# Down projections of both layers as seven products of half operands, with sums of the weights made beforehand

## The chip, the core and the metric

The kernel runs on one core of one Trainium2 chip. The metric is the device time of the whole program in microseconds; the median of several runs is compared. Single executions of one kernel agree within a few tenths of a per cent. Engines are named as the profile names them: PE (TensorE matmuls) with PEld (its weight loads), DVE (VectorE), ACT (ScalarE), POOL (GpSimd) and SP (SyncE, which here only issues DMA transfers).

## What is computed

One inference step of a two-layer network for two groups of requests, in float32: a prompt of 1024 tokens and 8 samples of 16 tokens, 1152 columns in all, with 1024 features. Layer 0 is an RWKV-7 time mixing, layer 1 a banded attention; behind each stands a SwiGLU feed-forward. Only the feed-forwards matter here:

```python
def swiglu(h, w_gate, w_up, w_down):
    return (jax.nn.silu(h @ w_gate) * (h @ w_up)) @ w_down
...
        h = modulate(rms_norm(x, p['norm_ffn'][l]), sh_f, sc_f)
        x = x + gt_f[:, None, :] * swiglu(h, p['w_gate'][l], p['w_up'][l], p['w_down'][l])
```

The inner width D_FF is 2816, that is 22 blocks of 128; `w_gate` and `w_up` are 1024 x 2816, `w_down` is 2816 x 1024. The modulations (shift, scale, gate of every sub-layer) come from `silu(c) @ w_ada + b_ada`.

## The kernel before

Features lie on the 128 partitions, tokens in the columns. The columns are split into two token groups, c = 0 with 512 and c = 1 with 640. A float32 product is made of three matmuls (`mm3`, line 143 issues each): both operands are split into a high part (ACT, L272) and the rest (DVE, L273), and high x high, high x rest and rest x high are added in PSUM. Weights are loaded raw by SP into a tile `rq` (five buffers), then split into a pair of tiles `w` (sixteen buffers, eight pairs).

The gate and up projections (`gate_up`, called from `ffn` for each of the 22 blocks f) already use seven products in place of eight: input features, tokens and output features (gate, up) are halved, sums of the weight quarters are formed on POOL (L1340 to L1343 in `strassen_weights`), and the products are added up on ACT, DVE and POOL (helper `add`, L1369), with L1376 and L1380 on ACT and L1383 and L1385 on DVE. Each product is a PSUM tile of 576 columns, 256 of group 0 and 320 of group 1, in half-groups of tokens. There are three such wide PSUM tiles (two `S`, one `PT`). The two results of a block, s0 and s1 (first and second half of each group's tokens), go to DRAM (`sd`, L1390).

The down projection (the second half of `ffn`) then runs over the 22 blocks in 11 pairs p, for c = 0 and 1 and for 8 blocks n of output features: six matmuls of 512 columns, or twelve of 320, give one PSUM tile that is added to a running sum in SBUF (L1436). The pair of blocks is read back from `sd` (L1411) and split; `w_down` is loaded and split in halves (L249). For the last pairs the gate and the residual are applied (L1170) in place of the addition, and the result is stored (L1440). In layer 0 the steps of `ada_steps` (modulations 12 to 27, loads at L260, matmuls from tile `h` with `scT`) run between the pairs, and `done` starts the next norm for each group as soon as it is ready; in layer 1 the down projection is the end of the program.

The engines' queues are in order. Which instruction stands where in each queue is decided when the program is built, by a scheduler with its own estimates; a tile with one buffer is handed on when its last reader has finished, a DMA included.

Of the kernel before, what the change touches and what calls it, by code (L numbers as in the profile page):

```python
# [8 lines left out]
F32 = mybir.dt.float32  # L9
F32R = mybir.dt.float32r  # L10
AF = mybir.ActivationFunctionType
ALU = mybir.AluOpType
# [64 lines left out]
def prep(i):  # L77
    i = {k: np.asarray(v) for k, v in i.items()}
    d = {}
    d["cst"] = _CST  # L80
    d["ti"] = _solver_identity()
    t = np.arange(384)
    rs = np.stack([t % 64 != 0, np.where(t < 256, t % 64, t % 16) != 0]).astype(np.float32)
    d["rs"] = np.ascontiguousarray(np.broadcast_to(rs[:, None], (2, 128, 384)))
    x = np.concatenate([i["x_prompt"][0], i["x_sample"].reshape(128, 1024)], 0)
# [5 lines left out]
    c = np.zeros((32, 1024), np.float32)  # L91
# [13 lines left out]
    st = i["state_wkv"][0].transpose(3, 1, 0, 2)  # L105
    st = st.reshape(64, 8, 2, 8, 64).transpose(2, 0, 1, 3, 4)
# [18 lines left out]
    q, u = np.arange(128)[:, None], np.arange(256)[None, :]  # L125
# [5 lines left out]
    for l in range(2):  # L131
        d[f"wg{l}"] = _tiles(i["w_gate"][l])
        d[f"wu{l}"] = _tiles(i["w_up"][l])
        d[f"wd{l}"] = i["w_down"][l].reshape(22, 128, 1024)
    return {k: np.ascontiguousarray(v) for k, v in d.items()}


# [8 lines left out]
class Trunk:  # L146
# [372 lines left out]
    def spill(self, n, b, f, t):  # L519
        self.nc.sync.dma_start(self.sp[b][n][:, :, f, :], t.rearrange("p (w t) -> p w t", t=128))  # L520
# [826 lines left out]
        yield put(a21)  # L1347
        yield put(a22)

    def gate_up(self, sd, B, W, cs):  # L1350

        nc = self.nc
        dve = nc.vector
        gp = nc.gpsimd
# [28 lines left out]
        dve.tensor_tensor(s1, s1, t5, ALU.mult)  # L1383
        add(dve, u3, product(3), u3)
        dve.tensor_tensor(s0, s0, u3, ALU.mult)  # L1385
        for h, s in enumerate((s0, s1)):
            for c in cs:
                o, n = 256 * c - n0, (256, 320)[c]
                t0 = 512 * c + n * h
                nc.sync.dma_start(sd[:, t0:t0 + n], s[:, o:o + n])  # L1390

    def ffn(self, l, B, W, part1, xsrc, dst, done):

        nc = self.nc
        sd = [self.dp.tile([128, 2, 1152], F32, name=f"sd{l}_{p}") for p in range(11)]
        self.gate_up(sd[0][:, 0], B, iter(W), (0,))
        for _ in part1:
            pass
        self.gate_up(sd[0][:, 0], B, iter(W), (1,))
        for f in range(1, 22):  # L1400
            self.gate_up(sd[f // 2][:, f % 2], B, self.strassen_weights(l, f, nc.vector if f == 1 else None), (0, 1))
        self.ada = self.ada_steps(range(12, 28), "acc", 1) if l == 0 else iter(())
        gate = 48 * l + 40
        acc, end = {}, iter(())
        act, W = {}, {}

        def begin(p):
            for c in range(2):
                w = (512, 640)[c]
                raw, hi, lo = (self.slot(c, dt)[:, :2 * w].rearrange("p (i t) -> p i t", i=2) for dt in (F32, F32R, F32R))  # L1410
                nc.sync.dma_start(raw, sd[p][:, :, self.cols(c)])  # L1411
                self.split(hi, lo, raw)
                act[p, c] = hi, lo
            W[p] = [self.halves(self.a[f"wd{l}"][f]) for f in (2 * p, 2 * p + 1)]
            self.step(7)

        for p, c in [(p, c) for p in range(9) for c in range(2)] + [(9, 1), (10, 1), (9, 0), (10, 0)]:
                if (p, c) not in act:
                    begin(p)
                if p == 0:  # L1420
                    acc[c] = self.feats(c)
                if p == 10:
                    st = self.sq_open()
                for n in range(8):
                    ns = slice(n % 4 * 128, (n % 4 + 1) * 128)
                    d, parts = self.pz(c)
                    for z, o, m in parts:
                        for i in range(2):
                            wh, wl = W[p][i][n // 4]
                            hi, lo = (act[p, c][h][:, i, o:o + m] for h in range(2))  # L1430
                            self.mm3(z, wh[:, ns], wl[:, ns], hi, lo, i == 0, i == 1)
                    y = acc[c][n]
                    if p == 0:
                        nc.scalar.activation(y, d, AF.Copy)
                    elif p <= 7:
                        nc.vector.tensor_tensor(y, y, d, ALU.add)  # L1436
                    else:
                        self.residual(512, n, gate, y, y, d)
                    if p == 10:
                        nc.sync.dma_start(dst[:, n, self.cols(c)], y)  # L1440
                        if l == 0:
                            self.sq_add(st, y, n < 6)
                    if p == 7:
                        x = self.ev("xin")[:, :y.shape[-1]]
                        nc.sync.dma_start(x, xsrc[:, n, self.cols(c)])
                        self.residual(512, n, gate, y, x, y)
                    next(end, None)
                if p == 10:
                    for _ in end:
                        pass  # L1450
                    end = done(c, acc[c], st)
        return end

    def dense(self, x2, x3, close):
# [531 lines left out]
```

## Time and profile before

| | us |
|---|---|
| median of 3 runs (3802.68 to 3817.41) | 3810.66 |
| the profiled execution | 3804.49 |
| its span | 3802.7 |
| busy in the span: PE | 3506.1 (92%) |
| DVE | 2263.6 (60%) |
| ACT | 1573.8 (41%) |
| POOL | 591.6 (16%) |

The busy shares are means over stages with different limits. The program has the time mixing up to about 1300 us, layer 0's gate/up stage from there to 1797 us, its down stage to about 2150 us, keys, values and attention to about 3000 us, layer 1's gate/up stage to 3520 us and its down stage to the end. Rows of a timeline give start, length, engine, line, operation, output<-inputs and shape, and in brackets the idle time before with what ended it. "DMA to landing" is the time from the start of the issue on SP to the moment at which the data are there.

### The profile page before, as it was taken

The numbers are of one execution on the slowest core, as the hardware profiler recorded it, in microseconds if no ns is written. First come the engines' busy times: TensorE is split into PE (matmuls) and PEld (weight loads), VectorE is DVE, ScalarE is ACT, GpSimd is POOL, SyncE is SP. The second block draws the span as 40 slices with busy tenths as digits, with TensorE's granted clock in tenths as the row PEclk, the third lists the DMA queues.
The fourth block names the chain that finished last, engine by engine and source line by source line (L and its number), as shares of the span: only waits on it lengthen the run. The fifth ranks groups of instructions, "written<-read, shape, count | busy, mean of one in ns | idle before, by whom it ended". The sixth has DMA issues, their size and how long they took to land.

```text
span 3802.7 us, 72100 instructions
## 1 busy us (share of the span) xinstructions
PE 3506.1 (92%) x28550; PEld 3098.0 (81%) x28550; DVE 2263.6 (60%) x4396; ACT 1573.8 (41%) x3006; POOL 591.6 (16%) x497
## 2 busy tenths in 40 slices
PE   5889989989999799999999899789889799999999
PEld 4777778777667699999888879667677799999898
DVE  4666667765445854554457742666565755545667
ACT  5545546544223533333311452556554533333310
POOL 0000000000011154453000100000000255444000
PEclk9887899899699899999999999899899899999999
DMA  5876776776665322224654122554565322222521
GB/s 212 236 216 170 207 220 184 201 203 201 192 197 176 113 84 76 76 73 157 221 177 172 64 71 92 153 151 155 152 203 178 120 78 71 76 75 96 171 86 66
DMA packets 426995, 554.01 MB, mean 146 GB/s; under 512 B 128385, under 2 KB 292737, under 8 KB 422177
## 3 DMA queue, kind: packets, MB, share of 16 engines
q1 hardware_dynamic: 351344, 450.68, 36.9%
q0 software_dynamic: 22224, 80.36, 6.9%
q10 hardware_dynamic: 53088, 18.36, 2.1%
q8 instruction: 225, 3.69, 0.4%
q14 instruction: 114, 0.93, 0.1%
HBM read 415.85 MB, written 133.40 MB: 144 GB/s over the span
## 4 chain that ended last, share of the span: by engine, by line
PE 69%; DMA 11%; DVE 10%; issue 4%; ACT 4%; SPq 1%; ACTq 0%; POOL 0%; DVEq 0%; POOLq 0%
PE S L143 32%; PE PT L143 15%; PE acc L143 12%; PE st L143 3%; PE O L143 2%; PE G L143 1%; DVE h L273 1%; PE aux L143 1%; PE PT L1811 1%; PE Y L143 1%; DMA TT<-Z 1%; DMA h<-out_kT 1%; DVE wlo L273 1%; DMA raw<-in_rw_o 1%; DMA h<-in_wo 1%
## 5 line engine op out<-in xcount | busy, mean ns | idle before, releaser
L143 PE MATMUL S<-h,w 128*128 128x320 f32 (+1 forms) x4944 | 689.7, 298 | 12.3 <-ACT h L272 4.8
L143 PEld LDWEIGHTS S<-h,w 128*128 128x128 f32 x4944 | 671.8, 191 | 18.4 <-ACT h L272 5.6
L143 PE MATMUL S<-h,wh 128*128 128x320 f32 (+1 forms) x2844 | 529.8, 338 | 15.9 <-DVE h L1170 6.8
L143 PE MATMUL acc<-mx,whi 128*128 128x384 f32 x1728 | 508.5, 372 | 32.7 <-ACT whi L272 13.0
L143 PEld LDWEIGHTS S<-h,wh 128*128 128x128 f32 x2844 | 456.1, 189 | 70.8 <-issue 12.3
L272 ACT ACTIVATE w<-rq 128x512 fp32r<-128x512 f32 x308 | 192.6, 629 | 515.1 <-PE S L143 201.1
L143 PEld LDWEIGHTS acc<-mx,whi 128*128 128x128 f32 x1728 | 337.6, 204 | 63.3 <-ACT whi L272 16.9
L273 DVE TENSOR_TENSOR w<-rq,w 128x512 fp32r<-128x512 f32 x308 | 267.8, 872 | 199.8 <-ACT w L272 199.0
L143 PE MATMUL PT<-h,w 128*128 128x320 f32 (+1 forms) x2448 | 347.6, 297 | 10.2 <-ACT h L272 4.7
L143 PEld LDWEIGHTS PT<-h,w 128*128 128x128 f32 x2448 | 332.1, 190 | 12.2 <-ACT h L272 5.1
L143 PE MATMUL acc<-mx,wlo 128*128 128x384 f32 x864 | 316.1, 366 | 8.3 <-DVE wlo L273 8.3
L1369 POOL TENSOR_TENSOR t<-t,t 128x576 f32<-128x576 f32 (+1 forms) x132 | 226.5, 1717 | 442.2 <-ACT t L1376 320.1
L143 PE MATMUL PT<-h,wh 128*128 128x320 f32 (+1 forms) x1428 | 284.2, 342 | 8.2 <-ACT h L1558 2.3
L143 PEld LDWEIGHTS PT<-h,wh 128*128 128x128 f32 x1428 | 231.7, 188 | 38.5 <-issue 5.0
L143 PEld LDWEIGHTS acc<-mx,wlo 128*128 128x128 f32 x864 | 175.0, 203 | 20.6 <-DVE wlo L273 12.9
L273 DVE TENSOR_TENSOR wlo<-raw,whi 128x1024 fp32r<-128x1024 f32 x114 | 139.1, 1221 | 84.9 <-ACT whi L272 83.8
L272 ACT ACTIVATE wh<-rq 128x512 fp32r<-128x512 f32 x124 | 74.8, 625 | 245.1 <-PE S L143 161.4
L273 DVE TENSOR_TENSOR h<-h,h 128x1024 fp32r<-128x1024 f32 (+4 forms) x112 | 122.3, 1106 | 88.3 <-ACT h L272 72.1
L272 ACT ACTIVATE whi<-raw 128x1024 fp32r<-128x1024 f32 x114 | 119.6, 1053 | 129.0 <-PE acc L143 62.6
L272 ACT ACTIVATE h<-h 128x1024 fp32r<-128x1024 f32 (+4 forms) x112 | 103.5, 935 | 159.8 <-DMA h<-sd 111.1
L1369 DVE TENSOR_TENSOR t<-S,t 128x576 f32<-128x576 f32 (+1 forms) x116 | 86.4, 744 | 122.7 <-PE S L143 122.7
L1436 DVE TENSOR_TENSOR h<-h,S 128x640 f32<-128x640 f32 (+1 forms) x150 | 111.9, 750 | 78.9 <-PE S L143 78.7
(444 smaller groups left out, 5625.0 us busy)
## 6 DMA issues: line engine op xcount, KB each, us to landing
h<-in_wada SPq DMA_DIRECT2D x64, 512.0 KB, 6.3
rq<-in_wg SPq DMA_DIRECT2D x88, 256.0 KB, 2.6
rq<-in_wu SPq DMA_DIRECT2D x88, 256.0 KB, 2.6
rq<-in_wd SPq DMA_DIRECT2D x88, 256.0 KB, 3.1
raw<-in_wada POOLq DMA_DIRECT2D x32, 512.0 KB, 5.0
kc<-in_ck SPq DMA_DIRECT2D x16, 1024.0 KB, 5.1
vc<-in_cv SPq DMA_DIRECT2D x16, 1024.0 KB, 6.0
sd<-t SPq DMA_DIRECT2D x88, 160.0 KB, 1.9
```

The costliest lines, as they stand in the source:

```text
L143: return nc.tensor.matmul(out, lhsT, rhs, start=start, stop=stop)
L272: self.nc.scalar.activation(hi, x, AF.Copy)
L273: self.nc.vector.tensor_tensor(lo, x, hi, ALU.subtract)
L1369: eng.tensor_tensor(out, x, y, ALU.add)
L1436: nc.vector.tensor_tensor(y, y, d, ALU.add)
L1811: nc.tensor.transpose(pt[:, j * 128:(j + 1) * 128], P[:, j * 128:(j + 1) * 128], self.C("ident"))
```

## The change

The down projection becomes seven products of halves as well: the inner dimension is halved into even and odd blocks of 128, the tokens into the halves that s0 and s1 already are, the output features into two times four blocks.

- The combinations of the s tiles are made on DVE when an odd block is ready (`odd` in `down_open`: four differences and sums), and all seven operands are stored to DRAM (`bd`), where s alone was stored before.
- The sums of the quarters of `w_down` are made in 64 pieces a layer (`down_sums`, three after each block): a load of 128 x 4 x 88, four POOL operations of 88 columns in place, a store to DRAM (`ws`). The tile has one buffer.
- The new function `down` runs seven products i by four blocks m of output features; each accumulates 11 blocks of the inner dimension, 33 matmuls of 256 columns and 33 of 320, into one wide PSUM tile. Results are kept and combined in SBUF where the running sums were. In layer 0 the last two products are run for group 1 first and then for group 0, so that the next norm can start for group 1; the modulations' weights pass through tiles of both groups' rings (before: group 0's).
- The sums of squares for layer 0's next norm are added on DVE throughout (before, six of eight on POOL).

```diff
-        d[f"wd{l}"] = i["w_down"][l].reshape(22, 128, 1024)
+        d[f"wd{l}"] = i["w_down"][l].reshape(11, 2, 128, 2, 4, 128).transpose(2, 3, 1, 4, 0, 5).reshape(128, 4, 5632)
...
         for f in range(1, 22):
-            self.gate_up(sd[f // 2][:, f % 2], B, self.strassen_weights(l, f, nc.vector if f == 1 else None), (0, 1))
+            self.gate_up(spill(f), B, self.strassen_weights(l, f, nc.vector if f == 1 else None), (0, 1))
+            for g in range(3 * f - 3, 64 if f == 21 else 3 * f):
+                self.down_sums(l, g)
+        return self.down(l, xsrc, dst, done)
...
+        def even(p):
+            def f(s0, s1, cs):
+                put(p, 0, s0)
+                held[:] = s0, s1
+            return f
+
+        def odd(p):
+            def f(s0, s1, cs):
...
+                e0, e1 = held
+                t6, t3 = (self.ev("t")[:, 0:576] for _ in range(2))
+                put(p, 2, s1)
+                nc.vector.tensor_tensor(t6, s1, e1, ALU.subtract)
+                put(p, 6, t6)
+                nc.vector.tensor_tensor(e1, e1, e0, ALU.subtract)
+                put(p, 4, e1)
+                nc.vector.tensor_tensor(e0, e0, t6, ALU.add)
+                put(p, 5, e0)
+                put(p, 1, s0)
+                nc.vector.tensor_tensor(t3, s0, e0, ALU.subtract)
+                put(p, 3, t3)
+            return f
...
+    def down_sums(self, l, g):
+
+        nc, gp = self.nc, self.nc.gpsimd
+        m, j = divmod(g, 16)
+        q = self.wq.tile([128, 4, 88], F32, tag="ws", name=self.nm("ws"), bufs=1)
+        nc.sync.dma_start(q, self.a[f"wd{l}"][:, :, g * 88:(g + 1) * 88])
+        gp.tensor_tensor(q[:, 3], q[:, 2], q[:, 3], ALU.add)
+        gp.tensor_tensor(q[:, 2], q[:, 0], q[:, 2], ALU.subtract)
+        gp.tensor_tensor(q[:, 0], q[:, 3], q[:, 0], ALU.subtract)
+        gp.tensor_tensor(q[:, 1], q[:, 1], q[:, 0], ALU.subtract)
+        nc.sync.dma_start(self.Ws[m][:, :, j * 88:(j + 1) * 88], q)
+
+    def down(self, l, xsrc, dst, done):
...
+        turns = [(i, (0, 1)) for i in (0, 1, 2, 4, 5)]
+        if l:
+            turns += [(i, (0, 1)) for i in (6, 3)]
+            self.ada = iter(())
+        else:
+            turns += [(i, (c,)) for c in (1, 0) for i in (6, 3)]
+            ring = (self.slot(k % 2) for k in range(1000))
+            self.ada = self.ada_steps(range(12, 28), "acc", 1, lambda: next(ring))
...
+        def operand(i, cs):
+            X = {}
+            for c in cs:
+                n = width[c]
+                X[c] = []
+                for j, nk in enumerate((4, 4, 3)):
+                    raw, hi, lo = (self.slot(c, dt)[:, :nk * n].rearrange("p (k t) -> p k t", k=nk) for dt in (F32, F32R, F32R))
+                    nc.sync.dma_start(raw, self.Bd[i][j][:, :, part[c]])
+                    self.split(hi, lo, raw)
+                    X[c].append((hi, lo))
+            return X
...
+        for i, cs in turns:
+            X = operand(i, cs)
...
+            for m in range(4):
+                W = weights(i, m)
+                d = self.wide()[:, 256:832]
+                for c in cs:
+                    for n, (j, k) in enumerate(ks):
+                        s = slice(k * 128, (k + 1) * 128)
+                        hi, lo = (X[c][j][h][:, k] for h in range(2))
+                        self.mm3(d[:, part[c]], W[j][0][:, s], W[j][1][:, s], hi, lo, n == 0, n == 10)
```

The order of the built program changes at three places that matter below. First SP's queue inside layer 0's gate/up stage: `in_wg` and `in_wu` are the weights of the next block, `sd` the results. Before, one block is

```order
L1335 DMA rq_17836<-in_wg 128x512
L1335 DMA rq_17838<-in_wg 128x512
L1335 DMA rq_17840<-in_wu 128x512
L1335 DMA rq_17842<-in_wu 128x512
L1390 DMA sd_6_14105<-t_17352 128x256
L1390 DMA sd_6_14105<-t_17352 128x320
L1390 DMA sd_6_14105<-t_17351 128x256
L1390 DMA sd_6_14105<-t_17351 128x320
```

and now (L1450 and L1455 are the load and the store of `down_sums`, L1411 stores an operand of the down products; an even block, where one is stored):

```order
L1450 DMA ws_19738<-in_wd 128x4x88
L1411 DMA bd_0_2_14101<-t_18448 128x576
L1455 DMA ws_3_14123<-ws_19738 512x1x88
L1335 DMA rq_19238<-in_wg 128x512
L1450 DMA ws_19745<-in_wd 128x4x88
L1335 DMA rq_19240<-in_wg 128x512
L1455 DMA ws_3_14123<-ws_19745 512x1x88
L1335 DMA rq_19242<-in_wu 128x512
L1450 DMA ws_19752<-in_wd 128x4x88
L1335 DMA rq_19244<-in_wu 128x512
L1455 DMA ws_3_14123<-ws_19752 512x1x88
```

Three loads and three stores stand between the four weight loads; in an odd block six L1411 stand where one is here. In layer 0 eight such load and store pairs stand ahead of block 1's weights, in layer 1 four; the other 56 and 60 stand in this pattern.

Second POOL's queue in the same stage. Before, a block is

```order
L1340 TENSOR_TENSOR rq_16705<-rq_16640,rq_16642 128x512
L1341 TENSOR_TENSOR rq_16640<-rq_16636,rq_16640 128x512
L1342 TENSOR_TENSOR rq_16636<-rq_16705,rq_16636 128x512
L1343 TENSOR_TENSOR rq_16638<-rq_16638,rq_16636 128x512
L1369 TENSOR_TENSOR t_16392<-t_16392,t_16393 128x576
L1369 TENSOR_TENSOR t_16392<-t_16392,t_16394 128x576
L1369 TENSOR_TENSOR t_16393<-t_16393,t_16395 128x576
```

and now it begins and goes on as

```order
L1342 TENSOR_TENSOR rq_18453<-rq_18522,rq_18453 128x512
L1451 TENSOR_TENSOR ws_19211<-ws_19211 128x88
L1452 TENSOR_TENSOR ws_19211<-ws_19211 128x88
L1343 TENSOR_TENSOR rq_18455<-rq_18455,rq_18453 128x512
L1453 TENSOR_TENSOR ws_19211<-ws_19211 128x88
L1454 TENSOR_TENSOR ws_19211<-ws_19211 128x88
L1451 TENSOR_TENSOR ws_19218<-ws_19218 128x88
L1452 TENSOR_TENSOR ws_19218<-ws_19218 128x88
L1453 TENSOR_TENSOR ws_19218<-ws_19218 128x88
L1454 TENSOR_TENSOR ws_19218<-ws_19218 128x88
L1369 TENSOR_TENSOR t_18180<-t_18180,t_18181 128x576
L1369 TENSOR_TENSOR t_18180<-t_18180,t_18182 128x576
```

with a third set of four and the last L1369 behind it, then the next L1340. One group's sums are cut by L1343, the next stand right behind, the third between the second and the third L1369.

Third DVE's queue in an odd block, from the multiplication that waits for POOL's last L1369 to the second split of the next weights. Before:

```order
L1383 TENSOR_TENSOR t_16152<-t_16152,t_16153 128x576
L1369 TENSOR_TENSOR t_16155<-S_16359,t_16155 128x576
L273 TENSOR_TENSOR w_16645<-rq_16636,w_16644 128x512
L1385 TENSOR_TENSOR t_16151<-t_16151,t_16155 128x576
L273 TENSOR_TENSOR w_16675<-rq_16638,w_16674 128x512
```

and now (L1433, L1435, L1437 and L1440 are the four operations of `odd`):

```order
L1383 TENSOR_TENSOR t_18180<-t_18180,t_18181 128x576
L1369 TENSOR_TENSOR t_18183<-S_18387,t_18183 128x576
L1433 TENSOR_TENSOR t_18414<-t_18180,t_17922 128x576
L273 TENSOR_TENSOR w_18720<-rq_18711,w_18719 128x512
L1385 TENSOR_TENSOR t_18179<-t_18179,t_18183 128x576
L1435 TENSOR_TENSOR t_17922<-t_17922,t_17921 128x576
L273 TENSOR_TENSOR w_18750<-rq_18713,w_18749 128x512
L1437 TENSOR_TENSOR t_17921<-t_17921,t_18414 128x576
L1440 TENSOR_TENSOR t_18415<-t_18179,t_17921 128x576
```

Two of the four stand ahead of the splits whose inputs L1342 and L1343 then overwrite, two behind them.

More of the change, by code (lines that the diff above doesn't have):

```diff
@@ L1348, in strassen_weights, with gate_up @@
         yield put(a22)
-    def gate_up(self, sd, B, W, cs):
+    def gate_up(self, put, B, W, cs):
         nc = self.nc
@@ L1385, in gate_up @@
         dve.tensor_tensor(s0, s0, u3, ALU.mult)
[L1386 to L1390, printed above, removed]
+        put(s0, s1, cs)
     def ffn(self, l, B, W, part1, xsrc, dst, done):
         nc = self.nc
-        sd = [self.dp.tile([128, 2, 1152], F32, name=f"sd{l}_{p}") for p in range(11)]
-        self.gate_up(sd[0][:, 0], B, iter(W), (0,))
+        spill = self.down_open(l)
@@ L1397, in ffn @@
+        self.gate_up(spill(0), B, iter(W), (0,))
         for _ in part1:
             pass
-        self.gate_up(sd[0][:, 0], B, iter(W), (1,))
+        self.gate_up(spill(0), B, iter(W), (1,))
         for f in range(1, 22):
-            self.gate_up(sd[f // 2][:, f % 2], B, self.strassen_weights(l, f, nc.vector if f == 1 else None), (0, 1))
-        self.ada = self.ada_steps(range(12, 28), "acc", 1) if l == 0 else iter(())
-        gate = 48 * l + 40
-        acc, end = {}, iter(())
-        act, W = {}, {}
@@ L1407, in begin @@
[L1407 to L1420, printed above, removed]
-                    acc[c] = self.feats(c)
[L1422 to L1446, printed above, removed]
@@ new lines, in ffn, with down_open, put, first @@
+            self.gate_up(spill(f), B, self.strassen_weights(l, f, nc.vector if f == 1 else None), (0, 1))
+            for g in range(3 * f - 3, 64 if f == 21 else 3 * f):
+                self.down_sums(l, g)
+        return self.down(l, xsrc, dst, done)
+    def down_open(self, l):
+        nc = self.nc
+        self.Bd = [[self.dp.tile([128, n, 576], F32, name=f"bd{l}_{i}_{j}") for j, n in enumerate((4, 4, 3))] for i in range(7)]
+        self.Ws = [self.dp.tile([128, 4, 1408], F32, name=f"ws{l}_{m}") for m in range(4)]
+        b12 = self.dp.tile([128, 576], F32, name=f"b12_{l}")
+        held = []
+        def put(p, i, t):
+            nc.sync.dma_start(self.Bd[i][p // 4][:, p % 4], t)
+        def first(s0, s1, cs):
+            cr = slice(256, 576) if cs[0] else slice(0, 256)
+            nc.sync.dma_start(self.Bd[0][0][:, 0, cr], s0)
+            nc.sync.dma_start(b12[:, cr], s1)
+        def even(p):
[5 more added lines that the diff above has]
+            def f(s0, s1, cs):
+                if p == 0:
+                    held[:] = (self.ev("t")[:, 0:576] for _ in range(2))
+                    nc.sync.dma_start(held[0], self.Bd[0][0][:, 0])
+                    nc.sync.dma_start(held[1], b12)
+                e0, e1 = held
[11 more added lines that the diff above has]
+            return f
+        return lambda f: first if f == 0 else (odd if f % 2 else even)(f // 2)
@@ L1447, in ffn @@
                     next(end, None)
-                if p == 10:
-                    for _ in end:
+            if l == 0 and i == 3:
+                for g in (self.ada, end):
+                    for _ in g:
                         pass
-                    end = done(c, acc[c], st)
+                end = done(cs[0], acc[cs[0]], sq[cs[0]])
         return end
```

65 lines of the change are left out of this document (added).

## The prediction

> **What bounds the kernel now.** I read the page first, then the busy time by stage, then one block of the two stages that the change touches. By stage (columns: length, busy time of PE, PEld, DVE, ACT, POOL with counts, granted clock, DMA share, GB/s):
>
> ```profile
> 3100.00:3300.00 200.00, 200.00 (x1504) 200.00 (x1503) 102.28 (x116) 63.74 (x107) 97.41 (x63) 1.00 0.22 74
> 3520.00:3802.00 282.00, 277.69 (x1588) 253.40 (x1586) 191.17 (x300) 54.19 (x73) 0.06 (x1) 1.00 0.32 106
> 1797.00:2115.00 318.00, 318.00 (x2130) 264.28 (x2129) 184.20 (x303) 68.29 (x95) 6.67 (x5) 1.00 0.53 187
> 2115.00:2155.00 40.00, 29.70 (x124) 22.87 (x124) 36.37 (x72) 17.58 (x32) 6.49 (x5) 0.96 0.20 73
> ```
>
> The first row is 200 us of layer 1's gate/up stage: PE never idle, clock full, 200/1504 = **133.0 ns** a matmul, where columns of 256 and 320 alternate. The second is layer 1's down stage, all but filled by PE too: 1588 matmuls of 512 and 320 columns, 4.3 us idle. The third is layer 0's down stage, with modulation matmuls between. So TensorE sets the pace in both, and the other engines matter only where the change makes one of them late.
>
> Layer 1's down stage begins and ends here (timeline; start, length, engine, line):
>
> ```profile
> 3520.35 1.55 PE L143 MATMUL PT<-h,wh 128*128 128x512 f32 x6
> 3798.85 0.75 DVE L1170 SCALAR_TENSOR_TENSOR h<-S,mod,h 128x512 f32<-128x512 f32 x1 [0.61 <-PE S L143]
> ```
>
> That is 278.5 us for 1584 matmuls, or 274.2 without the idle 4.3.
>
> One block f of the gate/up stage, on POOL and then on DVE:
>
> ```profile
> 1528.58 1.30 POOL L1340 TENSOR_TENSOR rq<-rq,rq 128x512 f32<-128x512 f32 x1
> 1529.96 1.69 POOL L1341 TENSOR_TENSOR rq<-rq,rq 128x512 f32<-128x512 f32 x1
> 1532.34 1.67 POOL L1342 TENSOR_TENSOR rq<-rq,rq 128x512 f32<-128x512 f32 x1 [0.69 <-DVE w L273]
> 1534.69 1.29 POOL L1343 TENSOR_TENSOR rq<-rq,rq 128x512 f32<-128x512 f32 x1 [0.68 <-DMA sd<-t]
> 1543.05 1.42 POOL L1369 TENSOR_TENSOR t<-t,t 128x576 f32<-128x576 f32 x1 [7.06 <-ACT t L1376]
> 1549.11 1.86 POOL L1369 TENSOR_TENSOR t<-t,t 128x576 f32<-128x576 f32 x1 [1.39 <-DVE t L1369]
> 1550.93 1.30 POOL L1340 TENSOR_TENSOR rq<-rq,rq 128x512 f32<-128x512 f32 x1
> ```
> ```profile
> 1528.66 1.83 DVE L1383 TENSOR_TENSOR t<-t,t 128x576 f32<-128x576 f32 x1 [1.32 <-POOL t L1369]
> 1530.41 0.74 DVE L1369 TENSOR_TENSOR t<-S,t 128x576 f32<-128x576 f32 x1
> 1531.08 1.11 DVE L273 TENSOR_TENSOR w<-rq,w 128x512 fp32r<-128x512 f32 x1
> 1532.12 0.74 DVE L1385 TENSOR_TENSOR t<-t,t 128x576 f32<-128x576 f32 x1
> 1532.87 1.69 DVE L273 TENSOR_TENSOR w<-rq,w 128x512 fp32r<-128x512 f32 x1
> ```
>
> A block takes 1550.93 - 1528.58 = **22.35 us** (168 matmuls by 133.0 ns is 22.34). L1342 waits for one DVE split (L273), L1343 for the next, L1383 for POOL's last L1369. POOL has some 10 us of waiting in a block, so it looks as if there were room.
>
> **The change, part by part.** *Down matmuls.* 528 of 512 columns and 1056 of 320 become 924 of 256 and 924 of 320 a layer. Their mean is that of the gate/up stage: 1848 x 133.0 = 245.8 us, against 274.2. That is -28.4 us a layer, **-57 us**. Layer 0 has the same matmuls at the same clock, so I take the same there.
>
> *Their feeding.* Seven products instead of eleven passes relieve DVE's additions; weight splits grow from 44 halves a layer to 84, in layer 0 to 108. One block of output features of one product takes 66 matmuls, 8.8 us, and needs three splits. By
>
> ```profile
> L272 ACT ACTIVATE w<-rq 128x512 fp32r<-128x512 f32 x308 | 192.6, 629 | 515.1 <-PE S L143 201.1
> L273 DVE TENSOR_TENSOR w<-rq,w 128x512 fp32r<-128x512 f32 x308 | 267.8, 872 | 199.8 <-ACT w L272 199.0
> ```
>
> these cost DVE 2.6 us, hidden under PE. Layer 0 is worse off at its end: the last two products run for one token group at a time, so their weights are loaded and split twice, and 24 splits (24 x 0.872 = 21 us of DVE) fall in the stretch that has the next norm too, where DVE was busy 36.4 of 40 us. PE has longer work there (8 x 33 matmuls of 256 columns, some 31 us, where 16 sums of six by 512 took 22), so I charge +10 of the 21; 0 if that work hides it, 20 if not.
>
> *The sums of weights (L1450 to L1455).* This is the term that decides. Each of 64 groups a layer is a chain: load 180 KB, four POOL additions of 88 columns, store 180 KB. The tile has one buffer, so the next load waits until the store has landed; and all of it stands in SP's and POOL's order between the weight loads and the additions that the block itself needs. The trace shows no such transfer and no such addition. For loads of 512 pieces L830 is the nearest row, for stores of small pieces L690 (384 pieces of 256 B; once in a quiet stretch, once over all):
>
> ```profile
> L830 SPq DMA_DIRECT2D BK<-sp_b x18: 585/612/627, 152.5 to 1088.9; - x18
> DMA to landing us min/median/max: 2.8/4.1/6.7
> ...
> L1335 SPq DMA_DIRECT2D rq<-in_wu x36: 327/328/328, 1364.4 to 1747.6; - x36
> DMA to landing us min/median/max: 2.4/2.5/3.8
> ...
> L690 SPq DMA_DIRECT2D sp_v<-e x6: 368/430/1433, 262.2 to 276.0; - x6
> DMA to landing us min/median/max: 1.9/2.3/2.9
> ...
> DMA to landing us min/median/max: 1.8/3.4/6.5
> ```
>
> Load: 2.8 us (L830's least; it stands in bursts of four in a stage with busy DMA engines, this stage has a share of 0.22), bounds 2.4 (the weight load of this very stage) and 4.1. Store: 2.3, bounds 1.8 and 3.4. For POOL's additions:
>
> ```profile
> L1299 POOL TENSOR_TENSOR h<-h,h x12: 735/904/3136, 2955.3 to 2970.6; 128x256 f32<-128x256 f32 x12
> L1340 POOL TENSOR_TENSOR rq<-rq,rq x40: 1292/1296/1719, 1337.3 to 3475.3; 128x512 f32<-128x512 f32 x40
> L467 POOL COPY hb<-shin x1: 295/295/295, 590.1 to 590.1; 128x64 f32<-128x64 f32 x1
> ```
>
> 735 ns at 256 and 1292 at 512 columns make a line of 2.18 ns a column plus 178 ns: 370 ns at 88, estimated; bounds 295 (the copy) and 735. With the 0.08 us between L1340's end and L1341, four take 1.8 us.
>
> POOL's order now gives one even block, from L1340: to L1342's end 5.4 us as above; two sums 0.9 (6.3); L1343 1.4 (7.7); two sums 0.9 (8.6); store and next load 2.3 + 2.8 + 0.2 for two wake-ups (13.9); four sums 1.8 (15.7); store and load 5.3 (21.0; the first two L1369 fit beside it); four sums 1.8 (22.8); the last L1369 1.5, then the next L1340: **24.3 us**. The third store and load lie beside L1369 to L1342 and cost nothing. In an odd block two of the four new DVE differences (0.74 each) precede the splits that L1342 and L1343 wait for, and the store waits on SP behind six spills for the last difference (0.7 more): **26.5**. Mean **25.4**, against PE's 22.35.
>
> Prefetched weights do not cover this: DVE is in order and stands at L1383 until POOL's late L1369 ends, so it empties PSUM late, and three wide tiles let PE run ahead by two products at most, some 5 us once a layer. SP's order puts 8 groups of layer 0 and 4 of layer 1 ahead of block 1's weights; 116 remain, 38.7 blocks of three. 38.7 x (25.4 - 22.35) = 118, less 2 x 5: **+108**. For the 12 chains ahead, between loads that the start of the stage needs, **+5** (0 where DVE is late there anyway, 15 if half are seen).
>
> *Spills.* Seven operands instead of one copy of s are 1.8 MB in odd blocks, at the 22% share covered; the DVE differences are counted. The tail after the last matmul (0.75 us and a store) stays alike.
>
> Sum: 3804.5 (the profiled execution; its span is 3802.7) - 57 + 10 + 108 + 5 = **3870 us**. The median of the three runs shown is 3810.7, 6 above that execution and within their spread; I shift nothing.
>
> One thing may lengthen the sums that no term has: L1383 took 1.83 us beside L1340, while L1385, of the same shape, took 0.74 with POOL idle. If half of a block's twelve sums stood 0.35 us behind a split, a block would be 2 us longer and the time 3870 + 38.7 x 2 = 3947, which is why my forecast's own band reaches up to 3960. The Trainium skill, page "SBUF — State Buffer", section "SBUF: two separate sides", has it as a rule, by which a VectorE operation with two SBUF inputs and a GpSimd operation that reads SBUF shut each other out for a whole instruction; L1383's row agrees.
>
> **Rivals.** (1) *The chains fit.* With a load of 2.4, a store of 1.8 and 295 ns a sum, two pairs and twelve sums shorten a block by 1.8 + 0.9 to 22.7, and 38.7 x 0.35 is all but covered by the 10: 3804.5 - 57 + 10 + 4 = **3761**, faster. For it: POOL idles 10 us a block now and SP has few issues. Against it: each must be at its least at once. It wins from a mean block below some 23.3 us.
> (2) *The chains nearly fit*, a block of 23.3 to 24.2: 3790 to 3823, no difference.
> (3) *Stores of 352-byte pieces are slow.* If each store first read what it overwrites, a load's 2.8 us would be added to each of two stores on the path: a block of 31 us, 38.7 x 8.65 - 10 + 5 - 47 = +283, **4087**. For it speaks only that no store of such pieces is in this stage; against it L690's 256-byte pieces land in 2.3. The Trainium skill, "DMA: Bandwidth & Descriptors", section "Specifications", has such a rule: transfers below 512 B make the DMA engine read, modify and write. L690 shows no sign of it.
> (4) *The products starve.* If each product but the first waited 3 us for its operand's tiles (four of fourteen slots are free), 12 x 3 = 36 more: **3906**. Against it: one turn of 8.8 us lies between the release of a tile and its need.
>
> **Numbers.** Forecast, 3823 to 3960: 0.47. (4): 0.07. (3) or other slow transfers, above 3960: 0.11. (2): 0.16. (1): 0.19. The range 3765 to 3985 leaves out about 0.1 at each end: its foot is rival 1, its head a block of 28.4 us, halfway from 25.4 to the 31.1 that loads of 4.1 and stores of 3.4 would give (those were taken among busier DMA engines; additions of 735 ns would add 4.4 more, far from the line). A measurement of this kernel cannot tell under 0.5% from no change. Faster 0.19, same 0.17, slower 0.64.
>
> **What would show it.** In the changed profile, blocks (L1340 to L1340) of 24 to 27 us, odd ones longer; fewer than 1400 matmuls in 200 us of gate/up; SP's waits led by L1450 for its own stores and L1455 for POOL; 128x88 additions near 0.37 us; down stages of about 250 us. Blocks of 22.4 us prove the loop wrong; loads near 2.4 and stores near 1.9 its sizes.

## The result and the profile after

The changed kernel takes **3957.16 us** (median of 4 runs, 3953.06 to 3970.34) against 3810.85 (4 runs): 1.0391 times as long, 95% interval 1.0359 to 1.0423. Slower, as forecast, and inside the range, but by 146 us where the forecast had 60. The profiled execution spans 3954.0 us, 151.3 more than the one of before.

Where they stand is read from rows that both timelines have. PE before (start, length, line, operation): a matmul of the mixing's last outputs; the norm's sums ahead of layer 0's feed-forward; the first gate/up matmul; the first matmul of the down stage; the first one of the norm of the keys (the keys' own products begin some 20 us earlier, beside the end of the down stage); the first gate/up matmul of layer 1. Its down stage begins at 3520.35, as shown above.

```profile
1247.29 0.69 PE L143 MATMUL acc<-mx,wlo 128*128 128x384 f32 x1 [0.90 <-DVE wlo L273]
1286.50 1.65 PE L143 MATMUL aux<-sqa,cst 128*128 128x384 f32 x2 [4.27 <-DVE sqa L311]
1290.61 5.04 PE L143 MATMUL S<-h,w 128*128 128x256 f32 x24 [2.46 <-DVE kk L333]
1797.25 1.93 PE L143 MATMUL acc<-h,scT 128*32 128x256 f32 x32
2163.51 0.70 PE L143 MATMUL acc<-ht,cst 128*128 128x320 f32 x2
3006.39 5.72 PE L143 MATMUL S<-h,w 128*128 128x256 f32 x24 [0.67 <-ACT w L272]
```

The same places after the change, with layer 1's first down product as the last row:

```profile
1255.72 0.69 PE L143 MATMUL acc<-mx,wlo 128*128 128x384 f32 x1 [0.90 <-DVE wlo L273]
1308.29 1.65 PE L143 MATMUL aux<-sqa,cst 128*128 128x384 f32 x2 [13.45 <-DVE sqa L311]
1312.40 5.21 PE L143 MATMUL S<-h,w 128*128 128x256 f32 x24 [2.46 <-DVE kk L333]
1897.84 8.95 PE L143 MATMUL PT<-h,w 128*128 128x256 f32 x66
2255.71 0.70 PE L143 MATMUL acc<-ht,cst 128*128 128x320 f32 x2
3103.89 3.23 PE L143 MATMUL S<-h,w 128*128 128x256 f32 x12 [2.17 <-ACT w L272]
3696.70 17.75 PE L143 MATMUL S<-h,w 128*128 128x256 f32 x132
```

The first L1340 on POOL parts the start of each gate/up stage from its blocks; before and after:

```profile
1337.32 1.29 POOL L1340 TENSOR_TENSOR rq<-rq,rq 128x512 f32<-128x512 f32 x1 [6.73 <-DMA rq<-in_wu]
3062.02 1.29 POOL L1340 TENSOR_TENSOR rq<-rq,rq 128x512 f32<-128x512 f32 x1 [8.34 <-DMA rq<-in_wu]
```
```profile
1374.21 1.29 POOL L1340 TENSOR_TENSOR rq<-rq,rq 128x512 f32<-128x512 f32 x1 [5.94 <-DMA rq<-in_wu]
3172.40 1.29 POOL L1340 TENSOR_TENSOR rq<-rq,rq 128x512 f32<-128x512 f32 x1 [5.87 <-DMA rq<-in_wu]
```

| stage | before | after | difference |
|---|---|---|---|
| to the first gate/up matmul | 1290.6 | 1312.4 | +21.8 |
| layer 0, to the first L1340 on POOL | 46.7 | 61.8 | +15.1 |
| layer 0, blocks | 459.9 | 523.6 | +63.7 |
| layer 0, down stage, to the norm of the keys | 366.3 | 357.9 | -8.4 |
| keys, values, attention | 842.9 | 848.2 | +5.3 |
| layer 1, to the first L1340 on POOL | 55.6 | 68.5 | +12.9 |
| layer 1, blocks | 458.3 | 524.3 | +66.0 |
| layer 1, down stage to the span's end | 282.4 | 257.3 | -25.1 |

Of the first 21.8 us, 8.4 had come up by the first row (1255.72 against 1247.29), ahead of the first addition of a chain at 1256.6. They are the mixing's spread: a run with no sums at all is 14.5 later there. The other 13.4 fall beside the chains: 9.2 are PE's longer wait for `sqa` (13.45 against 4.27), and the stretch from the first row to that wait took 39.1 us instead of 34.9 (34.9 without sums too). So the starts cost 13.4 + 15.1 + 5.3 + 12.9 = **46.7 us**, the blocks **129.7**, and the down stages give **33.5**. The 5.3 of the attention are inside the spread of that stage, 832 to 860 us in runs where no edit touched it.

Why the start waits is in the order on SP, in one POOL row and in one DVE row:

```profile
1286.82 0.57 SPq L1450 DMA_DIRECT2D ws<-in_wd  x1
1294.91 0.53 SPq L1455 DMA_DIRECT2D ws<-ws  x1
1297.31 0.57 SPq L1450 DMA_DIRECT2D ws<-in_wd  x1
1297.97 0.57 SPq L1204 DMA_DIRECT2D x<-e  x1
1298.59 0.42 SPq L1201 DMA_DIRECT2D rr<-in_x  x1
```
```profile
1289.71 3.81 POOL L1451 TENSOR_TENSOR ws<-ws 128x88 f32<-128x88 f32 x1 [5.81 <-DMA ws<-in_wd]
```
```profile
1301.99 0.48 DVE L1170 SCALAR_TENSOR_TENSOR e<-acc,mod,rr 128x256 f32<-128x256 f32 x1 [8.70 <-DMA rr<-in_x]
```

The residual input of the mixing's last outputs (L1201) stands on SP behind a store that waits for POOL and a load that waits for that store; DVE waits 8.70 us for it, and PE for DVE. The store at 1294.91 was late because the first addition of its chain took 3.81 us, ten times its usual 0.37, while DVE worked through its splits.

The blocks: windows of 200 us in both gate/up stages, then the two down stages (columns as in the prediction).

```profile
1500.00:1700.00 200.00, 180.02 (x1280) 177.41 (x1279) 100.53 (x112) 54.57 (x94) 115.82 (x142) 0.96 0.40 119
3300.00:3500.00 200.00, 179.23 (x1286) 176.35 (x1285) 100.81 (x113) 51.55 (x89) 121.05 (x147) 0.97 0.39 119
1897.00:2240.00 343.00, 320.49 (x2504) 286.12 (x2504) 177.25 (x327) 135.92 (x228) 1.90 (x2) 0.95 0.77 260
3697.00:3949.00 252.00, 247.87 (x1847) 246.19 (x1846) 133.88 (x224) 90.08 (x140) 1.80 (x1) 1.00 0.61 192
```

1280 matmuls where there were 1504: PE lost its full load. One even block on POOL (start, length, line, and in brackets the wait):

```profile
3309.09 1.26 POOL L1340 TENSOR_TENSOR rq<-rq,rq 128x512 f32<-128x512 f32 x1
...
3312.79 1.67 POOL L1342 TENSOR_TENSOR rq<-rq,rq 128x512 f32<-128x512 f32 x1 [0.69 <-DVE w L273]
...
3317.36 0.37 POOL L1454 TENSOR_TENSOR ws<-ws 128x88 f32<-128x88 f32 x1
3325.18 0.37 POOL L1451 TENSOR_TENSOR ws<-ws 128x88 f32<-128x88 f32 x1 [7.45 <-DMA ws<-in_wd]
...
3326.87 2.94 POOL L1369 TENSOR_TENSOR t<-t,t 128x576 f32<-128x576 f32 x2
3332.36 0.37 POOL L1451 TENSOR_TENSOR ws<-ws 128x88 f32<-128x88 f32 x1 [2.56 <-DMA ws<-in_wd]
...
3334.06 1.39 POOL L1369 TENSOR_TENSOR t<-t,t 128x576 f32<-128x576 f32 x1
3335.41 1.26 POOL L1340 TENSOR_TENSOR rq<-rq,rq 128x512 f32<-128x512 f32 x1
```

Sums, a wait of 7.45 us, sums, the block's own additions, a wait, sums: 26.3 us. POOL does nothing else while it stands at L1451, although L1369 is behind it. By the lists of waits over 3300 to 3500 (engine, line, for what: us, times, longest) this is POOL's only large one, and SP's are the two that the forecast named:

```profile
POOL ws L1451 <- DMA ws<-in_wd: 64.8, 15, 7.4
POOL rq L1342 <- DVE w L273: 8.2, 8, 1.4
```
```profile
SPq L1455 <- POOL ws L1454: 46.6, 23, 4.0
SPq L1450 <- DMA ws<-ws: 36.1, 23, 3.2
```

### The profile page after: what moved, and what is told of

Read it like the earlier page. It is cut to its first block, busy times and chain, and to the rows that moved or that the text cites. A ratio compares the mean times of both kernels' runs of the same rounds, so it can differ in the third digit from the quotient of the medians.

```text
span 3954.0 us, 74664 instructions
## 1 busy us (share of the span) xinstructions
PE 3505.3 (89%) x29078; PEld 3129.9 (79%) x29078; DVE 2255.6 (57%) x4380; ACT 1654.0 (42%) x3182; POOL 789.3 (20%) x999
## 4 chain that ended last, share of the span: by engine, by line
PE 40%; DMA 26%; DVE 10%; POOL 10%; issue 8%; ACT 4%; SPq 1%; ACTq 0%; POOLq 0%; DVEq 0%
PE S L143 14%; PE acc L143 10%; PE PT L143 7%; DMA ws<-in_wd 7%; DMA ws<-ws 6%; PE st L143 3%; POOL ws L1451 2%; POOL ws L1452 2%; PE O L143 1%; POOL ws L1453 1%; POOL t L1369 1%; DMA h<-bd 1%; DVE w L273 1%; POOL rq L1343 1%; PE aux L143 1%
## 5 line engine op out<-in xcount | busy, mean ns | idle before, releaser
L143 PE MATMUL S<-h,w 128*128 128x256 f32 (+1 forms) x7374 | 1065.8, 303 | 106.4 <-DVE t L1369 67.7
L143 PEld LDWEIGHTS S<-h,w 128*128 128x128 f32 x7374 | 1025.8, 195 | 135.4 <-DVE t L1369 77.4
L273 DVE TENSOR_TENSOR w<-rq,w 128x512 fp32r<-128x512 f32 (+1 forms) x500 | 378.9, 763 | 398.4 <-ACT w L272 390.7
L143 PE MATMUL PT<-h,w 128*128 128x256 f32 (+1 forms) x3714 | 550.3, 304 | 40.6 <-DVE t L1369 30.6
L272 ACT ACTIVATE w<-rq 128x512 fp32r<-128x512 f32 (+1 forms) x500 | 298.4, 610 | 680.1 <-POOL rq L1343 369.0
L143 PEld LDWEIGHTS PT<-h,w 128*128 128x128 f32 x3714 | 521.9, 196 | 53.1 <-DVE t L1369 34.9
L273 DVE TENSOR_TENSOR h<-h,h 128x1280 fp32r<-128x1280 f32 (+6 forms) x152 | 167.5, 1115 | 143.1 <-ACT h L272 137.1
L272 ACT ACTIVATE h<-h 128x1024 fp32r<-128x1024 f32 (+6 forms) x152 | 142.9, 950 | 193.4 <-DMA h<-bd 141.6
L1369 POOL TENSOR_TENSOR t<-t,t 128x576 f32<-128x576 f32 (+1 forms) x132 | 191.1, 1449 | 62.4 <-ACT t L1376 39.5
L1451 POOL TENSOR_TENSOR ws<-ws 128x88 f32<-128x88 f32 x128 | 82.1, 641 | 438.7 <-DMA ws<-in_wd 438.6
L143 PE MATMUL S<-h,wh 128*128 128x320 f32 (+1 forms) x744 | 144.4, 343 | 9.1 <-ACT wh L272 3.8
L143 PEld LDWEIGHTS S<-h,wh 128*128 128x128 f32 x744 | 120.5, 190 | 25.4 <-ACT wh L272 6.4
```

What stands on the lines that cost most here:

```text
L143: return nc.tensor.matmul(out, lhsT, rhs, start=start, stop=stop)
L272: self.nc.scalar.activation(hi, x, AF.Copy)
L273: self.nc.vector.tensor_tensor(lo, x, hi, ALU.subtract)
L1369: eng.tensor_tensor(out, x, y, ALU.add)
L1451: gp.tensor_tensor(q[:, 3], q[:, 2], q[:, 3], ALU.add)
```

## The experiments

Theory A: each group is a round trip (store lands, next load lands) through one tile, and POOL, in order, stands in it while its own additions wait. Rivals: POOL's added work and its collisions with DVE (F), SP's in-order waits (D), the odd blocks' differences and spills (B), the changed down stage (C), the spills of the first block (E).

| run | us | ratio to before, 95% interval | matmuls in 3300 to 3500 |
|---|---|---|---|
| no sums | 3789.4 | 0.9943 (0.9926 to 0.9960) | 1506 |
| additions alone | 3791.1 | 0.9953 (0.9932 to 0.9974) | 1506 |
| loads and stores alone | 3847.6 | 1.0102 (1.0067 to 1.0136) | 1405 |
| pinned, one buffer | 3964.8 | 1.0398 (1.0355 to 1.0442) | 1280 |
| 15 weight tiles | 3929.8 | 1.0300 (1.0265 to 1.0335) | 1309 |
| ... and 32 wide groups | 3926.7 | 1.0294 (1.0251 to 1.0336) | 1290 |
| ... and two buffers | 3886.5 | 1.0204 (1.0175 to 1.0234) | 1367 |
| two buffers, pinned | 3820.3 | 1.0008 (0.9991 to 1.0025) | 1506 |
| the same, from block 2 | 3796.9 | 0.9955 (0.9934 to 0.9975) | 1505 |
| the same, layer 1 alone | 3788.2 | 0.9937 (0.9915 to 0.9959) | 1507 |

**What the chains cost in all.**

```diff
-            for g in range(3 * f - 3, 64 if f == 21 else 3 * f):
-                self.down_sums(l, g)
...
-            src = self.Ws[m][:, {5: 0, 2: 1, 6: 2, 4: 3}[i]] if src is None else ...
+            src = {5: 0, 2: 1, 6: 2, 4: 3}[i] if src is None else src
```

> The sums of weights are left out: no loads, additions and stores of L1450 to L1455, and the four products that need sums read planes of w_down in their place. Theory A (chains: the sums alone cost the gate/up stages and their starts; the down stages gained as their matmuls say): blocks L1340 to L1340 back to 22.4 us, the gate/up starts back to those of the kernel before, so 3957 - 130 (loops) - 46 (starts) = 3781 us. Theory B (the odd blocks' four DVE differences and six spills are a good part of it): odd blocks stay at 24 us or more, 3820 us or above. Theory C (the changed down stage is slower than its matmuls say): 3810 or above with blocks of 22.4.

3789 us, all blocks 22.4 (odd ones too), layer 1's down stage 249 us as its matmuls say. So the chains cost 3957 - 3789 = **168 us**, B falls, and C holds for layer 0 alone: from the last L1340 to the norm of the keys (the row at 2163.51 above) it took 410.0 us, before 411.4. In other runs with the same down stage, and last blocks of 22.4 us, this stretch took from 401.8 to 408.4.

**Transfers alone, additions alone.** First without the four additions:

```diff
-        gp.tensor_tensor(q[:, 3], q[:, 2], q[:, 3], ALU.add)
...
-        gp.tensor_tensor(q[:, 1], q[:, 1], q[:, 0], ALU.subtract)
```

> The four additions of each group are left out; its load and its store stay. Theory A (each link of the chain counts, POOL's turn among them): without the sums three pairs of load 2.9 and store 2.4 are 16 us a block, less than PE's 22.35, so blocks of 22.4 to 23 us; the starts keep most of their loss, since the hoisted pairs still stand in SP's order: 3957 - 125 - 10 = 3822 us. Theory D (it is SP: its in-order waits for landings hold back weights and spills, whatever POOL does): blocks of 25 us or more, 3920 or above.

then without the transfers:

```diff
+        if g == 0:
+            nc.sync.dma_start(self.q, self.a[f"wd{l}"][:, :, 0:88])
...
+        gp.tensor_tensor(q[:, 3], q[:, 2], q[:, 1], ALU.add)
...
```

> The run without sums, with POOL's 256 additions of 128x88 a layer put back at the places in POOL's order that they have in the changed kernel (on a tile that is loaded once; their results are not used), and no load and no store of a group. Theory A (the round trip through memory in POOL's order is what costs): 12 additions of some 0.45 us beside POOL's own 10 us fit into a block of 22.35, blocks of 22.4 to 22.8 and 3789 to 3805 us. Theory F (POOL's time and its collisions with DVE): blocks of 24 us or more, 3850 or above.

58 us for the transfers alone (blocks of 22 to 28 until the groups, which this order packs four or five to a block, were done: more than A expected, less than D). For the additions alone it is 2 us, which is inside the scatter between sessions (the kernel before had medians of 3809.7 to 3815.2 in them). The window of that run and its additions (busy, mean ns):

```profile
3300.00:3500.00 200.00, 200.00 (x1506) 200.00 (x1506) 125.76 (x137) 64.20 (x108) 159.64 (x170) 1.00 0.28 97
```
```profile
L1456 POOL TENSOR_TENSOR ws<-ws 128x88 f32<-128x88 f32 x128 | 82.4, 643 | 5.4
```

POOL is busy 159.64 of 200 us and PE never idle. F falls for the blocks; ahead of them this run has three groups a layer where the changed kernel has twelve and seven, so it says little of the starts. 58 + 2 is not 168: the two parts cost little apart, and much where POOL's order holds both.

**The place of the chains.** `self.loaded` is the last weight load of block f; behind it on SP:

```diff
-            for g in range(3 * f - 3, 64 if f == 21 else 3 * f):
-                self.down_sums(l, g)
+            with self.tc.issue_after(self.loaded):
+                for g in range(3 * f - 3, 64 if f == 21 else 3 * f):
+                    self.down_sums(l, g)
```

> The groups of block f may not stand in SP's order ahead of block f's own weight loads, so none stands in the end of the mixing or of the attention; else as the changed kernel. Theory A (12 hoisted chains cost the starts 46 us): starts as in the kernel before, two more blocks' worth of chains in the loops, some 8 us: 3957 - 46 + 8 = 3919 us. Theory E (the starts lose through the first block's spills in two parts and their reload, L1415, L1416, L1428, L1429): no change, 3950 or above.

A miss: 3965. The mixing's end and the attention were freed of the chains (PE's wait for `sqa` was 4.23 us again), but the groups then stood beside block 2 and behind the last block, in the down stage. The start of layer 0 still took 61.7 us: there PE waited 11.1 us for DVE, and DVE 14.6 for a L1369 of POOL. While the blocks have no slack, a chain that is moved is paid for elsewhere.

**Two buffers.** They need room, so one weight tile goes; the control has that alone.

```diff
-        q = self.wq.tile([128, 4, 88], F32, tag="ws", name=self.nm("ws"), bufs=1)
+        q = self.wq.tile([128, 4, 88], F32, tag="ws", name=self.nm("ws"), bufs=2)
...
-            hi, lo = (self.wq.tile([128, 512], F32R, tag="w", name=self.nm("w"), bufs=16) for _ in range(2))
+            hi, lo = (self.wq.tile([128, 512], F32R, tag="w", name=self.nm("w"), bufs=15) for _ in range(2))
```

> Two buffers for the sums' tile, paid with one of the sixteen weight tiles. Theory A (the wait of the next load for the store, one buffer): two groups share a load and a store, 2.9 + 3.6 + 2.4 + 1.2 for issues is 10 us for two instead of 14, so blocks of 22.4 to 24 us and half of the starts' loss gone: 3957 - 38.7 x 3 - 20 = 3821, up to 3870 us. Theory F (POOL's time, 12 additions a block and their collisions with DVE, sets the block): blocks of 25.5 us or more, 3930 or above. Theory G (fifteen weight tiles are too few): blocks longer than 26.2, 3957 or above.

> The changed kernel with fifteen weight tiles instead of sixteen, one buffer for the sums as before: the control for the run with two buffers. If the weight tiles have no part, 3957 us (3945 to 3970), and all of the 71 us between 3957 and 3887 are the second buffer's; if fifteen are too few, above 3975.

The control alone gained 27 us, which nobody expected (its chains and spills stand in another order on SP; not followed further), the second buffer 43 more. But here the groups are crowded into the first eleven blocks of layer 0 and the first fourteen of layer 1, and ahead of them. Spread evenly, behind the block's loads:

> Two buffers (fifteen weight tiles) and the groups of a block behind its own weight loads in SP's order: three chains a block to the end, none ahead. Theory A (what costs is POOL standing at L1451 for a round trip of store and load): the next group's load is in flight while the sums run, so blocks of 22.4 to 23.5 and starts as without sums: 3800 to 3835, about 3815. If SP's in-order waits for POOL cost as much: 3860 or above.

```profile
3300.00:3500.00 200.00, 200.00 (x1506) 200.00 (x1505) 122.57 (x137) 62.95 (x107) 144.04 (x170) 1.00 0.49 146
```

1506 matmuls, with all loads, sums and stores in place. Now the place counts too: 3886.5 - 3820.3 = 66 us. From block 2 on:

```diff
-                for g in range(3 * f - 3, 64 if f == 21 else 3 * f):
+                for g in range(max(0, 64 * (f - 2) // 20), 64 * (f - 1) // 20):
```

> As two_pinned, with the groups from block 2 on instead of block 1 (3.2 a block). Theory A (two buffers hide the round trip; what is left of the 31 us above the run without sums is in the two starts, where chains stand beside the first two blocks' loads): starts as in the run without sums, loops within 10 us of it: 3795 to 3812, about 3803 us.

3797 us, 8 above the run without sums: **160 of the 168 us are gone**, by a second buffer and the place of the chains (27 of them the control with fifteen weight tiles had alone). The two starts take 48.2 and 54.1 us, where they took 46.7 and 55.6 before the change. POOL's waits over the same 200 us as above (the line has moved by one):

```profile
POOL ws L1452 <- DMA ws<-in_wd: 34.7, 19, 3.8
POOL t L1369 <- DVE t L1369: 12.4, 9, 1.7
```

It still waits, 34.7 us instead of 64.8, and that fits beside its work. SP's waits in the same window:

```profile
SPq L1456 <- POOL ws L1455: 31.4, 20, 3.2
SPq L1456 <- POOL ws L1453: 27.7, 6, 5.2
SPq L1451 <- DMA ws<-ws: 16.2, 10, 3.6
```

SP still stands 59.1 us at the stores for POOL (in the changed kernel 46.6, and 26.9 more there until a load had landed), and PE loses nothing: so it is not SP's waiting for POOL as such (D) that costs. Its wait for its own stores fell from 36.1 to 16.2.

**Half as many chains.** 176 columns instead of 88, one buffer:

> Fifteen weight tiles, and the sums in 32 groups of 176 columns a layer instead of 64 of 88, still one buffer. Theory A (a price by the chain, mostly landings: load 3.0, four additions of some 0.57, store 2.4): half as many chains, each some 1.2 times as long, so the 168 us above the run without sums fall to about 100: 3885 us. Theory H (the price goes with the bytes or the columns, by DMA or POOL throughput): little change, 3930 or above.

A miss: 3927, the control 3930. Half as many chains did not halve the price. POOL's wait at L1451, by its groups (count, busy and mean ns, idle before): after the change, and here.

```profile
L1451 POOL TENSOR_TENSOR ws<-ws 128x88 f32<-128x88 f32 x128 | 82.1, 641 | 438.7 <-DMA ws<-in_wd 438.6
```
```profile
L1451 POOL TENSOR_TENSOR ws<-ws 128x176 f32<-128x176 f32 x64 | 56.8, 887 | 296.7 <-DMA ws<-in_wd 296.6
```

There is less waiting for loads in all (369.7 in the control), but in layer 0 blocks alternated between 28.6 to 29.3 us and 23.3, and PE's own work, 22.35, is the floor. The order changed too: eleven wide groups, with the columns of 22, stand ahead of layer 0's first L1340 where the control has twelve narrow ones. So the run does not separate the number of chains from their place.

**Other places for the sums.** In the down stage, from two to four raw planes just ahead of the split:

```diff
+                elif i in (4, 5, 2):
+                    nc.gpsimd.tensor_tensor(raw, raw, q[1], ALU.add)
+                if i in (5, 2):
+                    nc.gpsimd.tensor_tensor(raw, raw, q[2], ALU.subtract)
...
```

> The sums move to the down stage: the products that need one load two to four planes of w_down beside each other, and POOL (for the fourth operand of the third product DVE too) adds them just ahead of the split; nothing goes through DRAM and the gate/up stage has no chain. Theory A (the whole loss was the chains' place and their round trip through one tile): blocks of 22.4 us, starts as with the sums left out, down of layer 1 some 252 to 260 us: 3789 to 3810 us, about 3797. Rival (the third and sixth products starve: five raw buffers hold one piece and its planes at a time, so each piece waits for 2.9 us of loads, two sums of 1.3 us and a split): 8 blocks by 3 pieces by some 3 us a layer, 3860 us or above.

3884.6 us: blocks of 22.4, but layer 1's down stage took 300 us, PE idle for 31.5 of them and waiting first for ACT's weight splits; the rival was right. With fewer modulation steps it was no better, 3895.7, and layer 0's stretch from the last L1340 to the norm of the keys 12.5 us longer (467.1), which was neither of the two answers expected:

> As fly, with two steps of the modulations instead of three after each block of a product in layer 0's down stage. If the waits of the modulation matmuls (for DVE's add, ScalarE's copy and the DMA, some 12 us of PE idle in that stage of the changed kernel) come from units standing too close, the stage is 5 to 12 us shorter than in fly; if they come from the one PSUM bank within a unit, no difference.

On POOL's own DMA queue (`gp.dma_start`), layer 0's in the mixing and layer 1's in the attention; then layer 1's alone:

> The chains leave the gate/up stages altogether: layer 0's (88 groups of 64 columns) run in the mixing and layer 1's (32 groups of 176) in the attention, with loads and stores issued by POOL itself, which is idle there. Theory A (a chain costs only where an engine that has other work waits in order behind it): the gate/up and down stages as in the run without sums, the mixing and the attention within 15 us of theirs: 3789 to 3810, about 3797 us. Rival (the additions and their DMAs slow DVE or the transfers there as well): mixing or attention longer by 30 us or more, 3820 or above.

> Layer 0's feed-forward as in the kernel before; layer 1's down projection by seven products, its sums in the attention as in early_s0 (tiles from the slots of group 0). If layer 1 gives its 26 to 29 us and layer 0 gave nearly nothing: 3810 - 27 + 3 = 3786 us, faster than both kernels. If the attention pays for the chains: 3800 or above.

3861.7 us, with 43 us more up to the first gate/up matmul and 27 more in the attention than without sums; and 3809.5, no gain (0.9992, 0.9979 to 1.0004), nor with tiles of the other group (3816.4). The attention took 866 us there instead of 843, a difference that is not certain: with an attention that no edit touched it varied from 832 to 860 between these runs. In layer 0's down stage, three groups to a pair:

> Layer 0's feed-forward as in the kernel before; layer 1's down projection by seven products, its sums (32 groups of 176 columns, slots of group 1) in layer 0's down stage, on POOL's own queue, which is idle there for 311 of 318 us. If the chains cost only where working engines wait behind them: 3810 - 28 + 3 = 3785 us. If POOL's additions hold up DVE, or the transfers the operand loads, as they seem to in the attention: 3800 or above.

3809.2 (0.9983, 0.9967 to 1.0000), with 425.9 us from the last L1340 to the norm of the keys instead of 411.4. None of these places took them for nothing.

**Layer 0's down stage.** Two parts of the change undone, without sums: the modulations' tiles, and

```diff
-            turns += [(i, (c,)) for c in (1, 0) for i in (6, 3)]
+            turns += [(i, (0, 1)) for i in (6, 3)]
```

> The run without sums (they are left out), with layer 0's modulations loading through the slots of group 0 alone, as in the kernel before. If layer 0's missing gain (its down stage is 1 us shorter than before where matmuls say 28) comes from the modulations' waits and this part of the change, the stage is shorter or longer by 5 us or more than in the run without sums (409.6 us from the last L1340 to the next norm's first matmul); else within 3.

> The run without sums, with layer 0's last two products for both token groups at once, as in layer 1: 24 weight splits fewer at its end, but the next norm of both groups after the last matmul. If the split turns cost the 10 us that my prediction charged, and the order of the groups hides little: 5 to 10 us shorter than 3789; if the early norm of group 1 is worth more than the splits, 10 us or more longer, 3800 or above.

410.3 and 404.7 us from the last L1340 to the norm of the keys, against 410.0; the whole runs took 3793.5 and 3796.8. The tiles do nothing that shows. The 5 us of the split turns are inside the 401.8 to 410.0 that the stretch takes in runs where this part is untouched, so a price of theirs is not shown. Why layer 0 gains so little stays open in the main; what the trace shows of it stands in the next section.

**A faster kernel.** Layer 0 as before, layer 1 as in the run from block 2 on:

> Layer 0's feed-forward as in the kernel before, layer 1 as in two_late (its fifteen weight tiles and two buffers in layer 1 alone). Theory A: layer 1's down stage gives 27 us, its gate/up stage takes back some 5 to 8: 3810 - 27 + 7 = 3790 us, faster than both kernels by half a per cent. If the attention ahead or the stage's start pays again: 3800 or above.

**3788.2 us**, 0.9937 (0.9915 to 0.9959): 0.6% faster than the kernel before, and faster than the changed one. From the run with both layers changed (0.9934 to 0.9975) it cannot be told apart. Layer 1's blocks and its down stage:

```profile
3300.00:3500.00 200.00, 200.00 (x1507) 200.00 (x1505) 116.68 (x135) 64.05 (x108) 152.97 (x178) 1.00 0.49 148
3518.00:3768.00 250.00, 249.22 (x1869) 248.81 (x1867) 137.43 (x227) 90.01 (x140) 3.82 (x2) 1.00 0.62 195
```

## Why the prediction was right in sign and wrong in size

The mechanism held: the sums' chains in POOL's and SP's order outweigh the shorter down stages. The terms of the forecast add up to +66 on the profiled execution, the measured ones to +151.3. The 85.3 between them, term by term:

- **For the 12 chains ahead, +5 (15 if half are seen); measured 46.7** (41.4 without the attention, whose share is inside its spread). This is the step that failed, by 41.7 us. The loads that stand behind such a chain on SP are the inputs of the mixing's last outputs, and of block 1. I had priced this stretch by asking whether DVE was late there anyway, not by what stands behind each waiting store. Nor did I ask what DVE does to the additions there: in the two starts they took 26 us more in all than at 0.374 us each, single ones 3.8 and 4.8 us. How much of the 46.7 that is, no run separates. As the pinned run shows, the price isn't saved by moving the chains, so long as the loop has no room; with two buffers and the groups from block 2 on it is gone.
- **For the gate/up loop, +108; measured 129.7**, 21.7 more. In layer 1 the mean block from block 4 on was 26.0 us against 25.4: odd ones 26.8 (26.5 forecast), even ones 25.2 (24.3). In the even block above, the order and the times are as forecast to the end of its fourth sum (8.6 us after L1340). Then the round trip took 7.45 us where the sum had 5.3: the load landed after 4.8 us, between two weight loads of 256 KB, where 2.8 was taken; a median load took 2.9.
- **For the down matmuls, -57, and layer 0's end, +10; measured -33.5**, 13.5 less gain. Layer 1 gave 25.1 of 28.4. Layer 0 gave 8.4 instead of 18.4, and what failed there is "the same matmuls at the same clock, so I take the same there". Its matmuls did gain: PE was busy 320.5 us, 345.5 before. But it stood idle for 22.5 of 343, where 7.5 of 353 were idle before, and the granted clock was 0.95 instead of 1.00. The same stage before, and three of PE's waits in it after (1897 to 2240):

```profile
1797.00:2150.00 353.00, 345.53 (x2244) 285.66 (x2242) 215.57 (x364) 83.73 (x122) 11.25 (x8) 1.00 0.50 177
```
```profile
PE acc L143 <- DVE mod L228: 5.4, 4, 2.9
PE acc L143 <- ACT h L222: 4.3, 5, 1.4
PE acc L143 <- DMA h<-in_wada: 2.5, 2, 1.5
```

So 12.2 us of the idle time are waits of the modulations' matmuls, which had none in that stage before and no term in the forecast. Why they come late, and what the lower clock adds, stays open.
- The mixing's spread, 8.4, was in no term: the execution profiled before lay 6 us under the median of its runs.

Of the sizes, the additions' medians were 0.37 to 0.38 us as estimated (0.37), the store 2.4 (2.3), the load 2.9 (2.8). That a block would be 2 us longer if half of its sums stood behind a split was half right: in the two loops the twelve additions of a block took 1.1 us more than at 0.374 each. The additions do meet with DVE: the 271 of 512 with less than 0.06 us of DVE's work beside them took 0.38 us at most, the other 241 0.65 in the mean. That agrees with the Trainium skill, "SBUF — State Buffer", section "SBUF: two separate sides"; but with 0.64 us for its first one the run with additions alone lost nothing in its blocks, where POOL had the room. Rival 3 is out: 352-byte stores landed in 2.4 us, with no sign of the read ahead of a write that the Trainium skill, "DMA: Bandwidth & Descriptors", section "Specifications", gives for pieces under 512 B. Rival 4 was not seen in layer 1, whose down stage filled PE for 247.87 of 252 us; in layer 0 PE waited twice for the splits of an operand, 5.1 us in all.

## What to carry to other kernels

An engine's free time is worth nothing to work that makes it stand in order for a round trip through memory: 512 additions were all but free (2 us) and their transfers cheap (58), but together on one buffer they cost 168 us. Before placing such work in a full loop, give it a second buffer, so that the next load is in flight while the sums run, and pin its place behind the loop's own loads; one of the two without the other gave back less than half. And for each wait put on a shared queue, list what stands behind it, above all at the seams between stages.

## What was not expected of the hardware

- Twice the bytes hardly lengthened a landing: loads of 352 KB took 3.6 us at the median where 176 KB took 2.9, stores 3.0 where 2.4. It agrees with the Trainium skill, "DMA: Bandwidth & Descriptors", section "Anatomy of one DMA — SWDGE (gpsimd) path", which puts most of a small transfer's time into a fixed part; these are SP's.
- One weight tile fewer made the kernel 27 us faster (3957 to 3930). The scheduler wrote another order for it; that the order alone does it is not shown. Comparisons of a few per cent between schedules need such a control.
- One POOL addition of 88 columns took up to 4.8 us beside DVE's work, where its median was 0.37.
